# Seven half products for eight in the gate and up blocks of a SwiGLU, with their sums on three engines

## The chip, the cores and the metric

One core of a Trainium2 chip runs the whole program. The metric is the device time of one execution in microseconds (us), as the median of several runs. The profile is of one execution of its own; the time from its first to its last instruction is called the span.

The engines go by the profile's names. PE is the matrix engine, and PEld its loading of the stationary operand, which runs beside the products. DVE is the vector engine, ACT the scalar engine with the activation functions, POOL is GpSimd, and SP issues the transfers (DMA). SBUF is the memory in which tiles of 128 partitions lie; PSUM holds the eight banks that PE writes its sums to, each 128 x 512 float32.

## What is computed

One decoder layer on 512 tokens of width 1024: a SwiGLU, a token mixer (short convolution and sparse attention side by side), a second SwiGLU, a final norm. Scale, shift and gate vectors come from a conditioning vector `c` by a matrix `w_ada`. All arithmetic is to the accuracy of float32.

```python
D_MODEL = 1024; SEQ = 512; D_FF = 2816
def _swiglu(h, w_gate, w_up, w_down):
    return (jax.nn.silu(h @ w_gate) * (h @ w_up)) @ w_down
# in the layer
mod = (silu(c) @ w_ada + b_ada).reshape(B, 9, D_MODEL)      # shift, scale, gate, three times
h = _modulate(_rmsnorm(x, g_ffn1), sh1, sc1)
x = x + 0.5 * gt1 * _swiglu(h, w1_gate, w1_up, w1_down)
h = _modulate(_rmsnorm(x, g_mix), sh2, sc2)
x = x + gt2 * _hybrid_mixer(h, ...)
h = _modulate(_rmsnorm(x, g_ffn2), sh3, sc3)
x = x + 0.5 * gt3 * _swiglu(h, w2_gate, w2_up, w2_down)
return _rmsnorm(x, g_final)
```

## The kernel before

Channels lie on the partitions: `x`, and `h` in eight blocks of 128 channels by 512 tokens. Each operand of a product is kept as a high and a low part (`hhi`, `hlo`; `whi`, `wlo`; `ghi`, `glo`), and `mm3` (L280) makes one product out of three: high by high, high by low, low by high.

The 22 blocks `f` of 128 hidden channels of a SwiGLU have a gate and an up column block each. Blocks 0 to 2 are made together as `h` comes, channel block by channel block, in products of 256 tokens (`first_group`, and `first_products` in the first SwiGLU). Every later one is made by two calls of `project` (L536), gate then up, each 8 channel blocks x 3 products of 512 tokens into one bank. `glu` (L593) then takes the silu on ACT, multiplies by the up bank on DVE (L600), and splits the result on ACT (L605) and DVE (L607). After blocks 0 to 10 the first half of the last product is made (`part`, 8 channel blocks of the output, each 11 x 3 products) and added to `x` (`first_half`, L628); then come blocks 11 to 21 and the second half. Of that second half the last two output blocks are made in halves of 256 tokens, first both for tokens 0 to 255, then both for the rest, so that the norm of the first half of the tokens runs under the products of the second.

Weights come in units of 128 x 1024: SP loads a unit to one of four `raw` tiles (L344), ACT makes `whi` of it (L366), DVE or POOL makes `wlo` = `raw` - `whi` (L355). There are four pairs of `whi` and `wlo`. Under the first SwiGLU the other seven conditioning vectors are made (`ada_loads`, `ada_sums`): 56 rows of 128 x 1024 of `w_ada` are loaded to three `araw` tiles, and each is scaled and added on DVE (L862, L865); four small products and two transposes on PE end a vector.

What stands in which order on each engine is decided when the program is built. `Plan` is a list scheduler: a task asks for an engine and a time, or for one of several (`low_part` asks for DVE, or for POOL at a tax), and the plan takes the task that could begin first, with ranks for ties. Its costs are the functions from L218 on. Each engine then runs its instructions strictly in that order, and waits where an operand is not there.

Of the kernel before, what the change touches and what calls it, by code (L numbers as in the profile page):

```python
# [19 lines left out]
P = 128  # L20
# [5 lines left out]
FH = FK // 2  # L26
# [14 lines left out]
# columns of the packed per-channel vectors  # L41
# [8 lines left out]
# columns of the packed constants  # L50
# [74 lines left out]
class Slots:  # L125
    """Tokens for memory that is used over and over."""
# [108 lines left out]
def c_ptt(n):  # L235
    return POOL, 0.25 + 2.0e-3 * n
# [19 lines left out]
def tile_hymba_layer(ctx: ExitStack, tc: tile.TileContext, xT, pos, cols_d, con_d, wa0, wa1, f1a, f1b, f1d,  # L256
# [1636 lines left out]
```

## Time and profile before

| what | value |
|---|---|
| median of 3 runs | 1082.68 us (1081.89 to 1084.97) |
| span of the profiled execution | 1081.2 us |
| PE busy | 1062.0 us (98%), 5417 products |
| DVE busy | 606.7 us (56%) |
| ACT busy | 409.9 us (38%) |
| POOL busy | 49.8 us (5%) |
| granted clock of PE, mean | 0.989 of full speed |
| transferred by DMA | 133.60 MB, mean 124 GB/s |

The stages by the trace: up to about 66 us the start with the first vectors and the first products, to about 418 us the first SwiGLU, to about 700 us the mixer, to 1071 us the second SwiGLU, and then the final norm. Durations of matrix products in the rows overlap, since they are pipelined: what one costs is the distance from its start to the next start. The same holds, to a smaller degree, for back to back instructions of DVE, whose rows overlap by some 0.08 us.

### The profile page before, as it was taken

To read this page: it belongs to the slowest core of one execution; us is meant where nothing else is said; L and a number is where in the kernel's file an instruction comes from. 1 tells how busy PE (TensorE), PEld (TensorE's weight loads), DVE (VectorE), ACT (ScalarE), POOL (GpSimd) and SP (SyncE) were. 2 spreads that over 40 slices of the span, in tenths; PEclk is the share of its full clock that TensorE was granted. 3 is DMA by queue.
4 is the path that set the end of the run, shared out by engine and by line. 5 is a ranking of instruction groups with operands and counts; after the bars stand their busy time and mean duration, and the time that the engine had idled before them with its cause. 6 is when DMAs were issued, how large, how long until landed. Compare 5 with 4: busy or idle time off the path is not lost.

```text
span 1081.2 us, 13889 instructions
## 1 busy us (share of the span) xinstructions
PE 1062.0 (98%) x5417; PEld 860.6 (80%) x5417; DVE 606.7 (56%) x1069; ACT 409.9 (38%) x713; POOL 49.8 (5%) x47
## 2 busy tenths in 40 slices
PE   8999999999999999999999999999999999999997
PEld 5777677788888889987777777998888888888887
DVE  4978888833333347499787786654333323333334
ACT  4552222212222233358756785334222122222321
POOL 0310000000000001012001010100000000000000
PEclk8999999999999999999999999999999999999998
DMA  9659989532222230443300003224333333322302
GB/s 333 243 191 326 315 322 327 176 96 85 92 98 98 98 103 16 131 125 122 127 25 28 13 14 96 92 83 132 94 89 91 98 98 98 94 86 93 98 20 78
DMA packets 40706, 133.60 MB, mean 124 GB/s; under 512 B 4704, under 2 KB 8032, under 8 KB 40000
## 3 DMA queue, kind: packets, MB, share of 16 engines
q1 hardware_dynamic: 40640, 132.71, 37.3%
q8 instruction: 42, 0.69, 0.3%
q14 instruction: 24, 0.20, 0.1%
HBM read 130.14 MB, written 2.10 MB: 122 GB/s over the span
## 4 chain that ended last, share of the span: by engine, by line
PE 88%; DVE 5%; DMA 4%; issue 1%; ACT 0%; SPq 0%; DVEq 0%; ACTq 0%
PE b L278 86%; DMA araw<-in_wa_dram 3%; PE b L1396 2%; DVE ada L865 1%; DVE afirst L736 1%; DVE wlo L355 1%; DMA x<-in_xT_dram 1%; DVE s L519 1%; DMA raw<-in_f1b_dram 0%; PE b L1291 0%; DVE afirst L733 0%; DVE v L393 0%; PE b L1241 0%; DVE afirst L728 0%; ACT hhi L523 0%
## 5 line engine op out<-in xcount | busy, mean ns | idle before, releaser
L278 PE MATMUL b<-hhi,whi 128*128 128x512 f32 (+1 forms) x1020 | 386.1, 379 | 0.0
L278 PE MATMUL b<-hlo,whi 128*128 128x512 f32 (+1 forms) x1020 | 379.0, 372 | 0.5 <-DVE hlo L525 0.4
L278 PE MATMUL b<-hhi,wlo 128*128 128x512 f32 (+1 forms) x1020 | 378.7, 371 | 0.0
L366 ACT ACTIVATE whi<-raw 128x1024 fp32r<-128x1024 f32 (+3 forms) x176 | 178.1, 1013 | 461.8 <-PE b L278 319.8
L355 DVE TENSOR_TENSOR wlo<-raw,whi 128x1024 fp32r<-128x1024 f32 (+3 forms) x162 | 191.2, 1180 | 218.4 <-ACT whi L366 213.0
L278 PEld LDWEIGHTS b<-hhi,whi 128*128 128x128 f32 x1020 | 192.3, 189 | 41.5 <-issue 6.7
L278 PEld LDWEIGHTS b<-hhi,wlo 128*128 128x128 f32 x1020 | 192.5, 189 | 36.6
L278 PEld LDWEIGHTS b<-hlo,whi 128*128 128x128 f32 x1020 | 192.7, 189 | 34.9 <-DVE hlo L525 1.2
L278 PE MATMUL b<-ghi,whi 128*128 128x512 f32 (+1 forms) x364 | 138.2, 380 | 0.0
L278 PE MATMUL b<-ghi,wlo 128*128 128x512 f32 (+1 forms) x364 | 137.4, 378 | 0.0
L278 PE MATMUL b<-glo,whi 128*128 128x512 f32 (+1 forms) x364 | 137.4, 378 | 0.0
L600 DVE TENSOR_TENSOR s<-sg,b 128x512 f32<-128x512 f32 x44 | 30.1, 686 | 106.6 <-PE b L278 105.8
L278 PEld LDWEIGHTS b<-ghi,whi 128*128 128x128 f32 x364 | 68.4, 188 | 14.7 <-issue 0.8
L278 PEld LDWEIGHTS b<-ghi,wlo 128*128 128x128 f32 x364 | 68.5, 188 | 14.0
L278 PEld LDWEIGHTS b<-glo,whi 128*128 128x128 f32 x364 | 68.5, 188 | 13.9
L865 DVE SCALAR_TENSOR_TENSOR ada<-araw,cact,ada 128x1024 f32<-128x1024 f32 x49 | 66.7, 1360 | 16.8 <-DMA araw<-in_wa_dram 16.1
L532 DVE SCALAR_TENSOR_TENSOR x<-b,mod,x 128x512 f32<-128x512 f32 (+1 forms) x30 | 19.1, 643 | 42.3 <-PE b L278 42.3
L450 ACT ACTIVATE s<-x 128x256 f32<-128x256 f32 (+1 forms) x41 | 19.4, 491 | 56.8 <-DVE x L532 53.7
L355 POOL TENSOR_TENSOR wlo<-raw,whi 128x768 fp32r<-128x768 f32 (+2 forms) x14 | 30.8, 2197 | 217.8 <-ACT whi L366 162.8
L605 ACT ACTIVATE ghi<-s 128x512 fp32r<-128x512 f32 x44 | 27.5, 631 | 15.7 <-DVE s L600 15.7
L523 ACT ACTIVATE hhi<-s,mod 128x256 fp32r<-128x256 f32 (+1 forms) x42 | 20.8, 533 | 31.5 <-DVE s L519 28.5
L1407 DVE TENSOR_TENSOR PT<-b,PT 128x384 fp32r<-128x384 f32 (+1 forms) x48 | 28.2, 598 | 5.0 <-ACT PT L1405 4.5
(238 smaller groups left out, 969.0 us busy)
## 6 DMA issues: line engine op xcount, KB each, us to landing
araw<-in_wa_dram SPq DMA_DIRECT2D x56, 512.0 KB
raw<-in_f1b_dram SPq DMA_DIRECT2D x38, 512.0 KB
raw<-in_f2b_dram SPq DMA_DIRECT2D x38, 512.0 KB
raw<-in_f1d_dram SPq DMA_DIRECT2D x22, 512.0 KB
raw<-in_f2d_dram SPq DMA_DIRECT2D x22, 512.0 KB
raw<-in_wib_dram SPq DMA_DIRECT2D x14, 512.0 KB
wfirst<-in_wa_dram SPq DMA_DIRECT2D x5, 1024.0 KB
raw<-in_wc_dram SPq DMA_DIRECT2D x8, 512.0 KB
```

Source lines behind the costliest of these rows:

```text
L278: nc.tensor.matmul(o, lhsT, rhs, start=start, stop=stop)
L355: (nc.vector if e == DVE else nc.gpsimd).tensor_sub(wlo_of[j][:, :n], raw_of[i][:, :n], whi_of[j][:, :n].bitcast(F32))
L366: nc.scalar.activation(whi_of[j][:, :n], raw_of[raw_at[u]][:, :n], AF.Copy)
L450: nc.scalar.activation(o[:, ts], x[d][:, ts], AF.Square)
L519: nc.vector.scalar_tensor_tensor(t, x[d][:, ts], am[:, s, d:d + 1], rb(), op0=OP.mult, op1=OP.mult)
L523: nc.scalar.activation(hhi[d][:, ts], t, AF.Identity, bias=sh)
L532: nc.vector.scalar_tensor_tensor(x[d][:, ts], bank_of[b][:, ts], gate, x[d][:, ts], op0=OP.mult, op1=OP.add)
L600: nc.vector.tensor_mul(scr_of[q], sg_of[k], bank_of[bu])
L605: nc.scalar.activation(ghi[j], scr_of[q], AF.Copy)
L865: nc.vector.scalar_tensor_tensor(a, w, cact[:, k:k + 1], a, op0=OP.mult, op1=OP.add)
L1396: nc.tensor.transpose(pt[:, w:w + P], Pr[t][:, kb * P:(kb + 1) * P], ident)
L1407: nc.vector.tensor_sub(pl[:, :w], pt[:, :w], ph[:, :w].bitcast(F32))
```

## The change

From block 6 on in the first SwiGLU and from block 5 on in the second, 33 blocks in all, gate and up are made together by `seven`. Split `h` into its even and odd channel blocks and into tokens 0 to 255 (A) and 256 to 511 (B): gate and up are then a product of a 2 x 2 by a 2 x 2 of half blocks, eight half products, which Winograd's form of Strassen's method makes with seven products and sums of operands and results. Each of the seven is 4 channel blocks x 3 parts, 12 products of 256 tokens.

- The sums of `h` (`build_t`, tiles `thi`, `tlo`) are made once for each SwiGLU.
- The sums of the weights (`sums`, `sum_parts`, tiles `wsh`, `wsl`, four half slots) are made for every block: four sums of 512, and three splits of 512 into parts.
- The sums of results (`collect` in `seven`) are one copy of 256 on ACT and five additions of 256 on DVE for every block.
- The last product is made in four groups of 6, 6, 5 and 5 blocks for two of 11, each of the first three added to `x` as a whole. One more block of gate and up is made before each.
- In `ada_sums` the rows of `w_ada` come as 112 halves of 512, with three `araw` tiles of half the size; ACT scales a half and DVE or POOL adds it, or DVE does both at once.
- In the plan, POOL's cost of a subtraction is raised from 0.25 + 2.0e-3 n to 0.3 + 2.3e-3 n, its tax for weight work from 0.5 to 2, and PE's cost of three products is now 3 x (0.1133 + 0.469e-3 (n - 256)). Two kept unit slots are made at the end of the second SwiGLU as well.

Removed comments are left out here; so are the classes and loops that only carry the new units.

```diff
-FH = FK // 2
+SIZES = (6, 6, 5, 5)
+PLAIN = (6, 6, 5)
+def _steps():
+    for g in range(len(SIZES)):
+        for f in range(max(GROUP[g], GRP), GROUP[g + 1]):
+            yield "f", f
+            if g and f == GROUP[g]:
+                yield "d", g - 1
+    yield "d", len(SIZES) - 1
...
 def c_ptt(n):
-    return POOL, 0.25 + 2.0e-3 * n
+    return POOL, 0.3 + 2.3e-3 * n
...
 def c_mm3(n):
-    return PE, 3 * max(n / 2370, 0.105)
+    return PE, 3 * (0.1133 + max(0, n - 256) * 0.469e-3)
...
+    def sums(p):
+        a, b = p.u, p.u + 1
+        yield loaded[a]
+        yield loaded[b]
+        ga, up = raw_of[raw_at[a]], raw_of[raw_at[b]]
+        E, O = slice(0, T), slice(T, 2 * T)
+        x = yield scr
+        s1 = scr_of[x]
+        e = yield c_tt(T), (*c_ptt(T), W_TAX)
+        either(e).tensor_add(s1, up[:, E], up[:, O])
+        e = yield c_tt(T), (*c_ptt(T), W_TAX)
+        either(e).tensor_sub(up[:, E], ga[:, E], up[:, E])
+        done(p.third)
+        go(R_W, sum_parts(p, "1", s1, scr, x))
+        yield made[a]
+        e = yield c_tt(T), (*c_ptt(T), W_TAX)
+        either(e).tensor_sub(ga[:, E], s1, ga[:, E])
+        p.freed(scr, x, give)
+        go(R_W, sum_parts(p, "2", ga[:, E], raws, raw_at[a]))
+        e = yield c_tt(T), (*c_ptt(T), W_TAX)
+        either(e).tensor_sub(ga[:, O], ga[:, O], ga[:, E])
+        go(R_W, sum_parts(p, "4", ga[:, O], raws, raw_at[a]))
+
+    def sum_parts(p, n, v, slots, at):
+        p.slot[n] = yield halves_
+        hi, lo = half(p.slot[n])
+        yield c_act(T)
+        nc.scalar.activation(hi, v, AF.Copy)
+        e = yield c_tt(T), (*c_ptt(T), W_TAX)
+        either(e).tensor_sub(lo, v, hi.bitcast(F32))
...
+        def build_t(e):
+            x0, x1 = (yield scr), (yield scr)
+            h0, h1 = scr_of[x0], scr_of[x1]
+            for o, d in ((h0, 2 * e), (h1, 2 * e + 1)):
+                q = yield c_tt(T), (*c_ptt(T), W_TAX)
+                either(q).tensor_add(o, hhi[d].bitcast(F32), hlo[d].bitcast(F32))
+            a0, b0, a1, b1 = h0[:, A], h0[:, B], h1[:, A], h1[:, B]
+            for o, v, w in ((a0, b0, a0), (b0, b1, b0), (b1, b1, a0), (a1, a1, b1)):
+                q = yield c_tt(T // 2), (*c_ptt(T // 2), W_TAX)
+                either(q).tensor_sub(o, v, w)
+            for i, x in enumerate((x0, x1)):
+                hi, lo = (v[e][:, i * T:(i + 1) * T] for v in (thi, tlo))
+                yield c_act(T)
+                nc.scalar.activation(hi, scr_of[x], AF.Copy)
+                q = yield c_tt(T), (*c_ptt(T), W_TAX)
+                either(q).tensor_sub(lo, scr_of[x], hi.bitcast(F32))
...
+        def seven(f):
...
+            def collect(by):
...
+                yield has[1]
+                yield c_act(T // 2)
+                nc.scalar.activation(v, X[:, A], AF.Copy)
+                done(has["copied"])
+                yield has[6]
+                yield c_tt(T // 2)
+                nc.vector.tensor_add(v, v, Y[:, A])
+                yield has[7]
+                yield c_tt(T // 2)
+                nc.vector.tensor_add(w, v, Y[:, B])
+                done(has["w"])
...
+                nc.vector.tensor_add(up[:, B], w, X[:, B])
+                done(has["up"])
...
+                nc.vector.tensor_add(up[:, A], v, Y[:, B])
...
+                nc.vector.tensor_add(X[:, B], v, X[:, B])
+                give(scr, q)
+                k = yield from silu(f, bx)
+                e = yield c_tt(T), (*c_ptt(T), W_TAX)
+                either(e).tensor_mul(up, up, sg_of[k])
+                give(sgs, k)
+                yield from parts(f, r)
...
+            yield made[a]
+            yield from product(X[:, A], unit(a, 0), first(0, A), True)
+            done(has[1])
...
+            yield from product(Y[:, A], summed("2"), t_of(2), True)
...
+            yield from product(Y[:, B], unit(b, 0), t_of(3))
...
+            yield from product(X[:, B], summed("1"), t_of(1))
...
+            yield has["copied"]
+            yield from product(X[:, A], unit(a, DK // 2), first(1, A))
+            free_unit(a)
+            yield has["w"]
+            yield from product(Y[:, B], unit(b, DK // 2), t_of(4))
...
+            yield has["up"]
+            yield from product(X[:, B], summed("4"), first(1, B))
...
-                nc.vector.tensor_scalar(a, w, cact[:, 0:1], None, op0=OP.mult)
+                yield ACT, c_act(T)[1]
+                nc.scalar.activation(a, w, AF.Copy, scale=cact[:, 0:1])
             else:
-                yield c_stt(D)
-                nc.vector.scalar_tensor_tensor(a, w, cact[:, k:k + 1], a, op0=OP.mult, op1=OP.add)
+                e = yield c_stt(T), c_act(T)
+                if e == DVE:
+                    nc.vector.scalar_tensor_tensor(a, w, cact[:, k:k + 1], a, op0=OP.mult, op1=OP.add)
+                else:
+                    nc.scalar.activation(w, w, AF.Copy, scale=cact[:, k:k + 1])
+                    e = yield c_tt(T), (*c_ptt(T), W_TAX)
+                    either(e).tensor_add(a, a, w)
```

How this stands on the engines is shown at three places, each by a piece of the order before and of the order after. A number behind a name is that of the buffer.

PE, in the middle of the first SwiGLU. Before, the end of one `project` and the start of the next, 512 tokens each:

```order
L278 MATMUL b0_63<-hlo7_120,whi3_96 128x512
L278 MATMUL b0_63<-hhi7_112,wlo3_100 128x512
L278 MATMUL b6_69<-hhi0_105,whi0_93 128x512
L278 MATMUL b6_69<-hlo0_113,whi0_93 128x512
L278 MATMUL b6_69<-hhi0_105,wlo0_97 128x512
L278 MATMUL b6_69<-hhi1_106,whi0_93 128x512
```

After, the end of the first of seven half products and the start of the second, with sums of `h` and of weights as operands:

```order
L753 MATMUL b6_69<-hhi4_109,whi2_95 128x256
L753 MATMUL b6_69<-hlo4_117,whi2_95 128x256
L753 MATMUL b6_69<-hhi4_109,wlo2_99 128x256
L753 MATMUL b6_69<-hhi6_111,whi2_95 128x256
L753 MATMUL b6_69<-hlo6_119,whi2_95 128x256
L753 MATMUL b6_69<-hhi6_111,wlo2_99 128x256
L753 MATMUL b1_64<-thi0_679,wsh0_687 128x256
L753 MATMUL b1_64<-tlo0_683,wsh0_687 128x256
L753 MATMUL b1_64<-thi0_679,wsl0_688 128x256
L753 MATMUL b1_64<-thi1_680,wsh0_687 128x256
L753 MATMUL b1_64<-tlo1_684,wsh0_687 128x256
L753 MATMUL b1_64<-thi1_680,wsl0_688 128x256
```

A block has 48 products of 512 tokens before and 84 of 256 tokens after.

DVE, in the middle of the first SwiGLU. Before, between the L600 of one block and that of the next, with most of the time on rows of `w_ada` (L862, L865):

```order
L600 TENSOR_TENSOR s4_75<-sg0_688,b0_63 128x512
L865 SCALAR_TENSOR_TENSOR ada0_661<-araw0_658,cact_101,ada0_661 128x1024
L607 TENSOR_TENSOR glo6_683<-s4_75,ghi6_672 128x512
L865 SCALAR_TENSOR_TENSOR ada0_661<-araw1_659,cact_101,ada0_661 128x1024
L865 SCALAR_TENSOR_TENSOR ada0_661<-araw2_660,cact_101,ada0_661 128x1024
L355 TENSOR_TENSOR wlo0_97<-raw0_89,whi0_93 128x1024
L862 TENSOR_SCALAR ada1_662<-araw0_658,cact_101 128x1024
```

After, part of one block: weight sums (L422 to L433), their low parts (L442), sums of results (L782, L785, L791), the product of up and silu (L803) and its low part (L722), and halves of `w_ada` (L1115):

```order
L429 TENSOR_TENSOR raw2_91<-s5_76,raw2_91 128x512
L1115 TENSOR_TENSOR ada0_661<-ada0_661,araw2_660 128x512
L803 TENSOR_TENSOR s3_74<-s3_74,sg1_678 128x512
L433 TENSOR_TENSOR raw2_91<-raw2_91 128x512
L782 TENSOR_TENSOR s4_75<-s4_75,b1_64 128x256
L722 TENSOR_TENSOR glo3_674<-s3_74,ghi3_668 128x512
L442 TENSOR_TENSOR wsl1_690<-s5_76,wsh1_689 128x512
L785 TENSOR_TENSOR s4_75<-s4_75,b1_64 128x256
L1115 TENSOR_TENSOR ada0_661<-ada0_661,araw0_658 128x512
L422 TENSOR_TENSOR s1_72<-raw1_90 128x512
L791 TENSOR_TENSOR s2_73<-s4_75,b0_63 128x256
```

Weight sums, result sums and the rows of `w_ada` now stand in turns in DVE's one queue.

POOL. Before, from the end of the start to the mixer, it has two subtractions under the first SwiGLU (the last two here), and next a memset of the mixer:

```order
L355 TENSOR_TENSOR wlo2_99<-raw2_91,whi2_95 128x768
L728 TENSOR_TENSOR afirst1_133<-afirst1_133 128x256 x2
L355 TENSOR_TENSOR wlo0_97<-raw0_89,whi0_93 128x1024
L355 TENSOR_TENSOR wlo3_100<-raw3_92,whi3_96 128x1024
L996 MEMSET swp0_2754 128x512
```

After, a piece of the first SwiGLU, in which it has 11 of 1024 and 20 of 512:

```order
L396 TENSOR_TENSOR wlo1_98<-raw1_90,whi1_94 128x1024
L422 TENSOR_TENSOR s2_73<-raw1_90 128x512
L396 TENSOR_TENSOR wlo3_100<-raw2_91,whi3_96 128x1024
L442 TENSOR_TENSOR wsl0_688<-s5_76,wsh0_687 128x512
L442 TENSOR_TENSOR wsl0_688<-raw3_92,wsh0_687 128x512
L396 TENSOR_TENSOR wlo1_98<-raw0_89,whi1_94 128x1024
L442 TENSOR_TENSOR wsl1_690<-s1_72,wsh1_689 128x512
L442 TENSOR_TENSOR wsl0_688<-raw1_90,wsh0_687 128x512
L396 TENSOR_TENSOR wlo3_100<-raw3_92,whi3_96 128x1024
```

About one low part of a unit and one or two of a weight sum have gone from DVE to POOL for every block in this stretch.

## Rows read from the trace of the kernel before

**Rows 1.** The page's first part: busy us (share of the span) and instructions.

```profile
PE 1062.0 (98%) x5417; PEld 860.6 (80%) x5417; DVE 606.7 (56%) x1069; ACT 409.9 (38%) x713; POOL 49.8 (5%) x47
```

**Rows 2.** Windows from:to, length: busy us (instructions) by engine, PEclk, DMA share, GB/s.

```profile
core 0: us, PE busy (x) PEld busy (x) DVE busy (x) ACT busy (x) POOL busy (x), PEclk, DMA share, GB/s
100.00:165.00 65.00, 62.70 (x280) 48.67 (x279) 54.80 (x54) 17.86 (x24) 2.58 (x1) 0.97 0.90 314
205.00:300.00 95.00, 95.00 (x409) 76.55 (x408) 35.79 (x42) 24.87 (x31) 0.00 (x0) 1.00 0.29 95
427.00:705.00 278.00, 277.61 (x1624) 221.78 (x1623) 216.62 (x545) 170.81 (x366) 27.09 (x22) 1.00 0.24 75
705.00:1066.00 361.00, 361.00 (x1731) 298.72 (x1731) 129.88 (x161) 102.36 (x132) 0.00 (x0) 1.00 0.29 88
```

**Rows 3.** Timeline of PE: start, duration, instruction; 512 tokens, then 256.

```profile
399.69 0.39 PE L278 MATMUL b<-ghi,wlo 128*128 128x512 f32 x1
...
402.03 0.28 PE L278 MATMUL b<-ghi,whi 128*128 128x256 f32 x1
...
402.94 0.28 PE L278 MATMUL b<-ghi,wlo 128*128 128x256 f32 x1
```

**Rows 4.** Timeline of PE near the end of the second SwiGLU.

```profile
1061.04 0.28 PE L278 MATMUL b<-ghi,whi 128*128 128x256 f32 x1
...
1061.98 0.28 PE L278 MATMUL b<-ghi,wlo 128*128 128x256 f32 x1
```

**Rows 5.** Groups by line and shape: operation, count | busy us, mean ns | idle before.

```profile
L355 DVE TENSOR_TENSOR wlo<-raw,whi 128x1024 fp32r<-128x1024 f32 x136 | 166.3, 1224 | 188.9 <-ACT whi L366 183.5 <-PE b L278 0.8
L865 DVE SCALAR_TENSOR_TENSOR ada<-araw,cact,ada 128x1024 f32<-128x1024 f32 x49 | 66.7, 1360 | 16.8 <-DMA araw<-in_wa_dram 16.1
L463 DVE TENSOR_TENSOR ssum<-ssum,s 128x256 f32<-128x256 f32 x18 | 7.6, 423 | 6.6 <-ACT s L450 6.1
```

**Rows 6.** Timeline of DVE, back to back instructions in the first SwiGLU.

```profile
84.88 0.68 DVE L600 TENSOR_TENSOR s<-sg,b 128x512 f32<-128x512 f32 x1
85.47 1.22 DVE L355 TENSOR_TENSOR wlo<-raw,whi 128x1024 fp32r<-128x1024 f32 x1
86.61 0.69 DVE L607 TENSOR_TENSOR glo<-s,ghi 128x512 fp32r<-128x512 f32 x1
87.21 2.60 DVE L865 SCALAR_TENSOR_TENSOR ada<-araw,cact,ada 128x1024 f32<-128x1024 f32 x2
89.73 1.22 DVE L355 TENSOR_TENSOR wlo<-raw,whi 128x1024 fp32r<-128x1024 f32 x1
```

**Rows 7.** Timelines of POOL and of DVE around POOL's two subtractions of the first SwiGLU.

```profile
76.19 2.40 POOL L355 TENSOR_TENSOR wlo<-raw,whi 128x1024 fp32r<-128x1024 f32 x1 [18.63 <-ACT whi L366]
119.07 2.58 POOL L355 TENSOR_TENSOR wlo<-raw,whi 128x1024 fp32r<-128x1024 f32 x1 [40.48 <-ACT whi L366]
...
76.62 3.05 DVE L865 SCALAR_TENSOR_TENSOR ada<-araw,cact,ada 128x1024 f32<-128x1024 f32 x1 [0.57 <-DMA araw<-in_wa_dram]
79.59 0.68 DVE L607 TENSOR_TENSOR glo<-s,ghi 128x512 fp32r<-128x512 f32 x1
...
118.09 4.64 DVE L865 SCALAR_TENSOR_TENSOR ada<-araw,cact,ada 128x1024 f32<-128x1024 f32 x2 [1.74 <-DMA araw<-in_wa_dram]
```

**Rows 8.** The same two engines in the mixer, where DVE's operation reads a bank.

```profile
679.22 1.87 POOL L355 TENSOR_TENSOR wlo<-raw,whi 128x768 fp32r<-128x768 f32 x1 [35.53 <-PE b L278]
...
679.18 2.85 DVE L532 SCALAR_TENSOR_TENSOR x<-b,mod,x 128x512 f32<-128x512 f32 x4 [2.48 <-PE b L278]
```

**Rows 9.** Groups of POOL: the smallest subtraction of weights.

```profile
L355 POOL TENSOR_TENSOR wlo<-raw,whi 128x640 fp32r<-128x640 f32 x2 | 3.1, 1566 | 21.1 <-ACT whi L366 21.1
```

**Rows 10.** Waits of DVE from 66 to 210: us in total, times, longest.

```profile
DVE ada L865 <- DMA araw<-in_wa_dram: 16.1, 20, 2.1
DVE ada L862 <- DMA araw<-in_wa_dram: 2.7, 3, 1.7
```

**Rows 11.** Timeline of DVE at the end of the first SwiGLU.

```profile
410.47 0.48 DVE L532 SCALAR_TENSOR_TENSOR x<-b,mod,x 128x256 f32<-128x256 f32 x1 [3.01 <-PE b L278]
412.22 0.16 DVE L483 TENSOR_SCALAR v<-b 128x2 f32<-128x2 f32 x1 [1.27 <-PE b L278]
...
415.23 1.25 DVE L519 SCALAR_TENSOR_TENSOR s<-x,am,b 128x256 f32<-128x256 f32 x3
```

More of the change, by code (lines that the diff above doesn't have):

```diff
@@ L353, in low_part, with half, either @@
         n, i, j = units[u].shape[-1], raw_at[u], w_at[u]
-        e = yield c_tt(n), (*c_ptt(n), POOL_TAX)
+        e = yield c_tt(n), (*c_ptt(n), W_TAX)
         (nc.vector if e == DVE else nc.gpsimd).tensor_sub(wlo_of[j][:, :n], raw_of[i][:, :n],
                                                           whi_of[j][:, :n].bitcast(F32))
-        give(raws, i)
+        if u not in pair_of or u != pair_of[u].u:
+            give(raws, i)
         done(made[u])
+    half_of, halves_ = [], Slots()
+    def half(i):
+        t, c = divmod(i, 2)
+        return tuple(v[:, c * T:(c + 1) * T] for v in half_of[t])
+    def either(e):
+        return nc.vector if e == DVE else nc.gpsimd
+    def sums(p):
[27 more added lines that the diff above has]
+        either(e).tensor_sub(lo, v, hi.bitcast(F32))
+        p.freed(slots, at, give)
+        done(p.made[n])
     def make_units():
@@ L362, in make_units @@
             yield loaded[u]
+            p = pair_of.get(u)
+            if p is not None and u == p.u:
+                go(R_W, sums(p))
+            elif p is not None:
+                yield p.third
             j = yield slots_of.get(u, ws)
@@ L602, in glu @@
             give(sgs, k)
-            j = yield gs[f % FH]
-            yield c_act(T)
-            nc.scalar.activation(ghi[j], scr_of[q], AF.Copy)
-            yield c_tt(T)
-            nc.vector.tensor_sub(glo[j], scr_of[q], ghi[j].bitcast(F32))
-            give(scr, q)
-            done(g_in[f])
-        def part(half, d, b, ts, keep=False):
-            for k in range(FH):
-                n = d * FH + k
-                if (half, n // 8) not in at:
-                    at[half, n // 8] = take_unit()
-                u = at[half, n // 8]
+            yield from parts(f, q)
@@ L617, in part @@
+        def part(g, d, b, ts, keep=False):
+            m = SIZES[g]
+            for k in range(m):
+                n = d * m + k
+                if (g, n // 8) not in at:
+                    at[g, n // 8] = take_unit()
+                u = at[g, n // 8]
                 yield made[u]
-                yield g_in[half * FH + k]
+                yield g_in[GROUP[g] + k]
                 yield c_mm3(ts.stop - ts.start)
-                mm3(bank_of[b][:, ts], cols(u, n % 8), (ghi[k][:, ts], glo[k][:, ts]), k == 0, k == FH - 1)
+                mm3(bank_of[b][:, ts], cols(u, n % 8), (ghi[k][:, ts], glo[k][:, ts]), k == 0, k == m - 1)
@@ L629, in first_half, with keep @@
             give(banks, b)
+        def keep():
+            for k in range(N_S):
+                yield halves_
+            for hi, lo in half_of:
+                whi_of.append(hi)
+                wlo_of.append(lo)
+                give(kept[s], len(whi_of) - 1)
         def main():
@@ L653, in main @@
                     b = yield banks
-                    yield from part(1, d, b, ts, True)
+                    yield from part(last, d, b, ts, True)
                     go(R_X, residual(d, b, gate[d], ts, norm))
-            for n in range(8, FH):
-                free_unit(at[1, n])
+            for n in range((DK - 2) * SIZES[last] // 8, SIZES[last]):
+                free_unit(at[last, n])
             done(end)
+        for e in range(DK // 2):
+            go(R_T, build_t(e))
         go(R_MAIN, main())
```

194 lines of the change are left out of this document (147 added, 47 removed).

## The prediction

> **What bounds the kernel now.** I read the busy shares first, then the windows by stage, then the distances between starts on PE and on DVE. PE is busy for 98% of the span [rows 1], and in both SwiGLUs it is busy without a gap: 95.0 of 95.0 us from 205 to 300, 361.0 of 361.0 us from 705 on, at a granted clock of 1.00 [rows 2]. Fewer products there should therefore shorten the end, as long as the other engines keep up. DVE has room in these windows (36 of 95 us, 130 of 361), but little from 100 to 165 us, where the rows of `w_ada` are added: 54.8 of 65 us, with the transfers at 90% [rows 2]. That stretch is where the change puts most of its new work, so it decides.
>
> **Products.** Ten products of 512 tokens lie between 399.69 and 402.03, 0.234 us each; the eight of 256 after them take 0.91 us, 0.114 each [rows 3]. Other stretches of 256 run slower: 1061.04 to 1061.98 is eight of them, 0.1175 each [rows 4]. A block goes from 48 x 0.234 = 11.23 us to 84 x 0.114 = 9.58 (gain 1.65) or to 84 x 0.1175 = 9.87 (gain 1.36). The 33 blocks give 54.5 or 44.9 us. What tells the two speeds apart I can't see in the rows, so I take the middle, 1.50 a block: 24 us in the first SwiGLU (16 blocks), 25.5 in the second (17). The last product in four groups has the same number of products, so PE pays nothing for it; its 32 more additions to `x` go to DVE.
>
> **DVE in the first SwiGLU.** From start to start, DVE takes 1.14 us for 1024, 0.60 for 512 (85.47 to 86.61 to 87.21) and half of 2.52/2 = 1.26 for a half row scaled and added at once, 0.63 [rows 6]. For 256 I take the mean of 0.42 less the overlap of 0.08 that 1024 shows (1.22 against 1.14): 0.34 [rows 5, 6]. An addition to `x` is 2.85/4 = 0.71 [rows 8]. In the order after, I counted the stretch from block 7 to block 17, with one group of the last product in it. DVE has 20 of 1024, 130 of 512, 13 half rows, 54 of 256 and 9 additions to `x`: 22.8 + 78.0 + 8.2 + 18.4 + 6.4 = 133.8 us, and nine single operations for the rotary tables, some 4 us (estimate, below the 0.60 each). PE has 11 x 9.58 + 144 x 0.234 = 139 us there. So DVE alone is full, at 138 of 139 us, and the plan could only get there by giving POOL 8 of 1024 and 13 of 512.
>
> **What POOL's share costs.** The rows speak against counting it as free. POOL ran a subtraction from 76.19 to 78.59; DVE's L865, next at 76.62, took 3.05 us for a usual 1.3, and DVE's following start was at 79.59, a full operation after POOL's end. The same happened at 119.07: two L865 took 4.64 us for 2.5 [rows 7]. DVE waits, then, until POOL is through. Where DVE reads a bank it doesn't: four L532 at 679.18 ran in 2.85 us under POOL's 1.87 [rows 8].
>
> The Trainium skill, "SBUF — State Buffer", section "Who interferes with whom", has this as a rule: a DVE instruction with two SBUF inputs and a GpSimd instruction that reads SBUF exclude each other for the whole instruction, whichever came first, and a DVE instruction with at most one SBUF input outside its two-port modes is free. By that rule the sums here, which nearly all read two SBUF tiles, gain nothing from going to POOL; the trace's 3.05 us at 76.62 agrees.
>
> POOL's 1024 takes 2.40 us when it runs first [rows 7]; 640 takes 1.57 [rows 9], so 512 some 1.3 (estimate on the line through both). In the stretch: 8 x 2.40 + 13 x 1.3 = 36 us. DVE's operations that read a bank are 18.4 + 6.4 = 25 of its 138 us, 18%, and can pass under POOL; so I put 82% of the 36 on DVE's queue, 30 us, which PE then waits for. DVE may be ahead by half a block (four weight slots and four half slots are two blocks' at most), 5 us: 25 us of stall. Ends: half of POOL's time hidden and the same lead, 13; all of it and no lead, 36. Before block 7 the account is even: blocks 3 to 5 ask 29 + 11 us of DVE and POOL against 33 of PE, the group behind them gives that back. After block 17 DVE has room (28.8 against 38 us for the last four blocks), but a stall once paid isn't returned. If the 256 products are the slow ones, the stall shrinks by as much as PE loses.
>
> **The second SwiGLU** has no rows of `w_ada`, and POOL gets 15 operations. At its start the sums of `h` meet blocks 3 and 4 and the first seven: 4 of 1024, 34 of 512 and 20 of 256 are 31.8 us of DVE, with 2 x 2.4 + 4 x 1.3 = 10 of POOL, against 31.9 of PE. I charge 6 us (2 to 10). Later the six blocks 7 to 12 ask 47.4 us of DVE and 4 of POOL against 57.5: covered, with 6 us to spare.
>
> **Ends of the SwiGLUs.** The norm of tokens 0 to 255 runs under the products for the other half: two output blocks of 11 x 3 x 0.1175 = 3.9 us, 7.8 in all, now 5 x 3, 3.5 in all: 4.2 us less cover. The chain behind it took 410.47 to 415.23, 4.8 us, before `h` could be built [rows 11]. At the first end PE then waits for some 3 us; at the second, where the norm's first half and the last stores lie closer together, I take 1.5. Both from 0 to 4.
>
> **Waits inside a block.** Of the seven products, the sixth and the seventh wait for sums on DVE that begin two products earlier, 2.3 us; two additions of 0.34 fit unless a 1.14 or a POOL lock is in front. I charge 2 us over all blocks (0 to 6). Mixer code is the same; the plan's changed costs may order it otherwise. It has PE at 277.6 of 278 us by the modelled ends, with DVE at 217 [rows 2]: 0, from -4 to 4.
>
> **Sum**, against the profiled span of 1081.2: -49.5 + 25 + 6 + 4.5 + 2 = -12, 1069.2. The median lies 1.5 us above that span: 1071. The measurement can tell a change of over 0.3%, 3.2 us. The forecast's own range takes the ends together: from -54.5 + 13 + 2 + 3 = -36.5 to -44.9 + 36 + 10 + 7 - 10 (slow products hide a part of the stall) = -2: 1046 to 1081.
>
> **Rivals.**
> 1. POOL's work is hidden after all, for instance since DVE often waits for something else in that time. Then the stall in the first SwiGLU is DVE's alone (138 against 139, some 3 us), and 2 in the second: -49.5 + 5 + 6.5 = -38, with fast products -43: 1038 to 1046. For: POOL is the smaller of the two. Against: [rows 7], every time. 0.15.
> 2. Slower: a full DVE queue that waits for `w_ada`. Before, its L865 and L862 waited 18.8 us for transfers, nearly all that L865 ever waited [rows 5, 10], and PE felt little of it since DVE had room. Now a half row passes from DMA to ACT to DVE with half as many bytes in flight, and behind a late one stand the low parts and weight sums that PE's next product needs. If these waits come again and nothing covers them, they are added whole: -12 + 19 = 7, 1090. It turns slower once over 12 us of them reach PE. Against: ACT had 18 of 65 us to do there [rows 2], and the faster half of `w_ada`'s time now has longer to run. 0.17.
> 3. In between, within 3.2 us of before: the stall at its upper end, some of those waits. 0.13.
> 4. That the products don't get shorter: each of 256 has a weight load of its own. Within [rows 3] they did run at 0.114 with one load each, so this has no chance of its own.
>
> **How the numbers follow.** The forecast has 0.55, rival 1 0.15, so faster 0.70; same 0.13; slower 0.17. The range leaves out some 0.12 below and 0.08 above: 1043 to 1092.
>
> **What would show it.** Right: PE gaps in the first SwiGLU of about 25 us, before products that wait for L396, L442 or the additions of `collect`; the second SwiGLU about 15 us shorter than before, with its gaps at its start; DVE operations of 0.60 that last 1.5 to 2.5 us wherever POOL runs. Wrong: POOL and DVE overlapping on two SBUF inputs (rival 1); DVE idle before L1115 or L1111 with ACT or DMA as the releaser (rival 2); products of 256 at over 0.12.

## The result, and the profile after

The changed kernel takes 1090.95 us (median, 1089.57 to 1092.42), the kernel before, run beside it, 1083.83. The ratio is 1.0072, 95% interval 1.0052 to 1.0091: slower, where 1071 and faster were forecast. The profiled execution has a span of 1090.6 us for 1081.2.

Page, first part, after (for [rows 1]):

```profile
PE 1040.3 (95%) x6533; PEld 900.1 (83%) x6533; DVE 861.9 (79%) x1565; ACT 559.8 (51%) x969; POOL 117.9 (11%) x79
```

PE is busy for 22 us less, but the span is longer: it now idles. In what follows f6 is block 6, a pair is a block whose gate and up are made together by `seven`, and a group is one of the four parts of the last product. Stages, from the first product of each to the first of the next, in us; "undisturbed" is the time of the same products where nothing waits. In the first SwiGLU blocks 0 to 2 take products of 256 tokens for their first two channel blocks alone; the first row begins with the first product of 512, which still belongs to them:

| stage | before | after | undisturbed |
|---|---|---|---|
| first SwiGLU, first product of 512 to the last product's end | 382.8 | 395.3 | |
| of it f6 (first pair) | | 17.8 | 9.96 |
| of it f7 to f12, a group, f13 to f17 | | 77.6 + 34.6 + 58.5 | 59.8 + 33.6 + 49.8 |
| of it f18 to f21 | | 39.8 | 39.8 |
| from there to the second SwiGLU's first product (the mixer) | 281.1 | 284.7 | |
| second SwiGLU | 371.0 | 363.4 | |
| of it f5 and f6 (first pairs) | | 31.4 | 19.9 |
| of it f7 to f21 | | 59.8 + 49.8 + 39.8 | the same |

A pair, undisturbed, takes 9.96 us, a block before 11.2. Windows after (for [rows 2]; from:to, length, busy us of PE, PEld, DVE, ACT, POOL, then PEclk, DMA share, GB/s):

```profile
101.10:118.90 17.80, 13.36 (x85) 12.32 (x83) 13.41 (x21) 11.52 (x17) 0.00 (x0) 0.81 0.70 235
159.40:236.90 77.50, 69.05 (x525) 65.26 (x524) 74.26 (x107) 46.07 (x71) 25.09 (x12) 0.93 0.57 189
271.50:330.10 58.60, 53.68 (x432) 52.00 (x431) 55.57 (x82) 35.67 (x57) 16.73 (x8) 0.97 0.61 202
772.20:803.60 31.40, 22.70 (x170) 22.29 (x169) 23.55 (x33) 13.76 (x21) 4.19 (x3) 0.84 0.30 101
837.20:897.00 59.80, 59.80 (x506) 59.80 (x505) 49.78 (x80) 30.35 (x43) 7.64 (x3) 1.00 0.31 107
```

From f7 to f17 DVE is busy nearly all the time (74.3 of 77.5, 55.6 of 58.6), time in which it waits for POOL inside an operation included. Where no row of `w_ada` passes, last line, it has 49.8 of 59.8 us, and PE never waits. What PE waits for, over the whole span (us, times, longest):

```profile
PE b L753 <- DVE s L785: 8.4, 6, 3.0
PE b L300 <- DVE ada L1115: 7.7, 7, 1.8
PE b L753 <- DVE wsl L442: 6.7, 2, 6.0
PE b L753 <- ACT s L778: 4.7, 3, 3.7
```

L785 is `collect`'s second sum, L442 a low part of a weight sum. The waits are short, but the longer ones cost more than their length. After the 2.95 us at 291.68 the products start 0.11 us apart until 293.21, and 0.21 from there; the granted clock of 291.68 to 295.50 is 0.69, so part of it ran at the lower of the two levels, 1.2 GHz for 2.4 (PE's timeline):

```profile
291.68 0.39 PE L753 MATMUL b<-thi,whi 128*128 128x256 f32 x1 [2.95 <-DVE s L785]
291.90 0.28 PE L753 MATMUL b<-tlo,whi 128*128 128x256 f32 x1
...
293.80 0.41 PE L753 MATMUL b<-hhi,wsl 128*128 128x256 f32 x1
294.02 0.41 PE L753 MATMUL b<-hhi,wsh 128*128 128x256 f32 x1
```

Added over all starts of f7 to f12, 11.3 us are gaps and 5.4 us such doubled distances.

On the other engines three things stand in front of these waits. First, POOL and DVE exclude each other, as in [rows 7]: a subtraction of 0.60 lasts 1.79 beside POOL's.

```profile
175.35 1.54 POOL L442 TENSOR_TENSOR wsl<-raw,wsh 128x512 fp32r<-128x512 f32 x1 [1.37 <-ACT wsh L440]
175.66 1.79 DVE L433 TENSOR_TENSOR raw<-raw 128x512 f32<-128x512 f32 x1
```

Second, in f6 PE's last wait is for ACT's queue. The fourth product waits for ACT's copy of the first result (L778). The first product had ended at 102.6, but the copy stands behind a row of `w_ada`, for which ACT waits on the DMA (compare [rows 10]), and behind three other operations:

```profile
106.72 0.72 ACT L1113 ACTIVATE araw<-araw,cact 128x512 f32<-128x512 f32 x1 [1.19 <-DMA araw<-in_wa_dram]
107.35 0.58 ACT L713 ACTIVATE sg<-b 128x512 f32<-128x512 f32 x1
107.83 1.04 ACT L457 ACTIVATE whi<-raw 128x1024 fp32r<-128x1024 f32 x1
109.35 0.63 ACT L720 ACTIVATE ghi<-s 128x512 fp32r<-128x512 f32 x1 [0.48 <-DVE s L730]
109.88 0.36 ACT L778 ACTIVATE s<-b 128x256 f32<-128x256 f32 x1
...
110.30 0.58 PE L753 MATMUL b<-thi,wsh 128*128 128x256 f32 x1 [3.66 <-ACT s L778]
```

Third, at the second SwiGLU's start two of POOL's operations hold up DVE in a row, L433 and then L442, so that the low part at 782.18 reaches PE 6 us late:

```profile
775.36 2.35 POOL L396 TENSOR_TENSOR wlo<-raw,whi 128x1024 fp32r<-128x1024 f32 x1 [2.83 <-ACT whi L457]
775.40 2.85 DVE L433 TENSOR_TENSOR raw<-raw 128x512 f32<-128x512 f32 x1
...
779.31 1.75 DVE L442 TENSOR_TENSOR wsl<-s,wsh 128x512 fp32r<-128x512 f32 x1
...
782.18 0.68 DVE L442 TENSOR_TENSOR wsl<-raw,wsh 128x512 fp32r<-128x512 f32 x1
...
782.92 0.58 PE L753 MATMUL b<-thi,wsl 128*128 128x256 f32 x1 [6.04 <-DVE wsl L442]
```

### The profile page after: what moved, and what is told of

Its sections match the earlier page's. It is cut to its first block, busy times and chain, and to the rows that moved or that the text cites. A ratio compares the mean times of both kernels' runs of the same rounds, so it can differ in the third digit from the quotient of the medians.

```text
span 1090.6 us, 17104 instructions
## 1 busy us (share of the span) xinstructions
PE 1040.3 (95%) x6533; PEld 900.1 (83%) x6533; DVE 861.9 (79%) x1565; ACT 559.8 (51%) x969; POOL 117.9 (11%) x79
## 4 chain that ended last, share of the span: by engine, by line
PE 59%; DVE 8%; issue 2%; DMA 1%; ACT 1%; SPq 0%; ACTq 0%; DVEq 0%
PE b L300 38%; PE b L753 19%; PE b L1646 2%; DVE wlo L396 1%; DMA araw<-in_wa_dram 1%; DVE s L700 1%; DVE tlo L706 1%; DVE blkf L1357 1%; DVE glo L722 0%; DVE s L696 0%; DVE wsl L396 0%; DMA raw<-in_f1d_dram 0%; PE b L1541 0%; DVE wsl L442 0%; DVE raw L429 0%
## 5 line engine op out<-in xcount | busy, mean ns | idle before, releaser
L300 PE MATMUL b<-hhi,whi 128*128 128x512 f32 (+1 forms) x492 | 175.3, 356 | 2.2 <-ACT hhi L614 2.1
L300 PE MATMUL b<-hlo,whi 128*128 128x512 f32 (+1 forms) x492 | 169.8, 345 | 1.0 <-DVE hlo L616 0.9
L300 PE MATMUL b<-hhi,wlo 128*128 128x512 f32 (+1 forms) x492 | 169.4, 344 | 0.0
L300 PE MATMUL b<-ghi,whi 128*128 128x512 f32 x320 | 128.1, 400 | 1.3 <-ACT ghi L720 1.3
L300 PE MATMUL b<-glo,whi 128*128 128x512 f32 x320 | 127.2, 398 | 0.8 <-DVE glo L722 0.8
L300 PE MATMUL b<-ghi,wlo 128*128 128x512 f32 x320 | 127.2, 397 | 0.0
L300 PEld LDWEIGHTS b<-hhi,whi 128*128 128x128 f32 x492 | 92.5, 188 | 17.8 <-issue 3.5
L300 PEld LDWEIGHTS b<-hlo,whi 128*128 128x128 f32 x492 | 93.1, 189 | 12.0 <-DVE hlo L616 2.2
L300 PEld LDWEIGHTS b<-hhi,wlo 128*128 128x128 f32 x492 | 92.4, 188 | 12.3
L753 PE MATMUL b<-thi,whi 128*128 128x256 f32 x264 | 76.8, 291 | 8.5 <-DVE s L785 8.4
L1115 DVE TENSOR_TENSOR ada<-ada,araw 128x512 f32<-128x512 f32 x87 | 69.2, 796 | 15.1 <-ACT araw L1113 15.1
```

Source lines behind the costliest of these rows:

```text
L300: nc.tensor.matmul(o, lhsT, rhs, start=start, stop=stop)
L753: nc.tensor.matmul(o, u, v, start=start and not e and not i, stop=e == DK // 2 - 1 and i == 2, skip_group_check=not start)
L1115: either(e).tensor_add(a, a, w)
```

## Experiments: what fills DVE

Theory A: POOL's exclusion of DVE makes the stall. Theory B: DVE has more to do than fits beside the products, wherever it is done. Theory C: the waits for rows of `w_ada` make it.

**POOL does no weight work.**

```diff
-W_TAX = 2
+W_TAX = 1000
```

> GpSimd takes none of the weights' work any more (its planned cost there is put out of reach); DVE does all of it, products and blocks stay as changed. Theory A (a GpSimd operation on two SBUF inputs and a DVE operation of that kind cannot run side by side, so GpSimd's share is paid on DVE with interest): in the stretch of the pairs f7 to f12 DVE was busy for 73.7 of 77.5 us, 15.7 of it longer than its own operations last elsewhere, while GpSimd had 12 operations; on DVE these would be some 12 to 17 us of 512-wide rows' time halved, about 8 to 10 us. So DVE's load falls to about 66 to 68, the stretch to about the same (from 77.5), that of f13 to f17 from 58.5 to 50 to 52, and the start of the second SwiGLU by 3 to 5 us: 1066 to 1074. Theory B (DVE is too full and GpSimd relieves it): DVE takes 8 + 6 + 8 us more in these three stretches and the kernel is slower, 1103 to 1113. Theory C (the stall is the wait for the rows of w_ada through ACT): 1088 to 1094.

Measured: 1087.18 us, 1.0037 (1.0019 to 1.0056) of before; the interval just meets that of the change. The profile is of an execution of 1083.8 us, one of the faster of ten. Windows of f6, f7 to f12 and f13 to f17, and, from f7 to f17, what PE waited for, and what DVE waited for most (us, times, longest):

```profile
107.80:118.90 11.10, 10.99 (x93) 10.23 (x92) 8.62 (x14) 8.05 (x13) 0.00 (x0) 1.00 0.82 273
153.70:230.30 76.60, 66.05 (x525) 64.15 (x524) 68.06 (x117) 50.03 (x78) 0.00 (x0) 0.93 0.63 200
264.90:326.70 61.80, 54.31 (x442) 52.61 (x441) 55.92 (x95) 38.94 (x61) 0.00 (x0) 0.94 0.57 180
```

```profile
PE b L753 <- DVE wsl L442: 18.0, 6, 5.8
DVE s L782 <- PE b L753: 11.9, 8, 2.7
```

f7 to f17 takes 173.0 us for 170.7. So A fails as the cause: without POOL nothing excludes DVE, and the stall is the same. A's figure for DVE's load from f7 to f12 did come out, 68.1 us for 66 to 68, but the stretch took 76.6. B fails with its number too: POOL was no relief. What it took from DVE it gave back as waiting. C's 1088 to 1094 is the nearest; the next runs test it. DVE's own work from 153.7 to 326.7 is 157.7 us (68.1, 33.7 in the group between, 55.9), beside 143.2 us of undisturbed products. That load is about half of the 29.8 us lost (an estimate, 157.7 less 143.2). For the rest of the time DVE itself idles, 15.3 us, mostly in front of a sum of results (L782) that waits for PE, while PE waits for a low part (L442) further back in DVE's queue; and the clock is at 0.93 and 0.94. No run changed the order in DVE's queue alone, so how much of the stall is load and how much is order stays open. The second SwiGLU's first pairs do run in 19.9 us for 31.4, but its plain blocks lose 5.1 (27.5 us for 22.4).

**Without the sums of `w_ada`**, and, apart from it, **without the sums of the pairs**.

```diff
-            if k == 0:
+            if k and k < DK - 1:
+                pass
+            elif k == 0:
```

Of the eight rows of a group the middle six are loaded, but not added.

> As changed, but of the rows of w_ada that pass through DVE and ACT in the first SwiGLU only the first and the last of the eight of each group are summed (so the modulations are other numbers; loads and reductions stay). DVE's load in f7 to f12 falls by about 18 of 27 additions of 0.69 to 0.9 us, some 14 to 20 us, and in f13 to f17 by about 14. Theories A and B alike: no stall is left in the pairs of the first SwiGLU (59.8 for 77.5, 49.8 for 58.5, 9.96 for the 17.8 of f6): 1055 to 1062; A alone would leave a few us where GpSimd still works beside DVE. If the pairs' stall has to do with TensorE's own speed or the halves' buffers: 1085 or more.

Measured: 1086.03 us. The total misses the 1055 to 1062 by far, and by its number falls to the last alternative, that the stall has to do with PE or the buffers; the stage speaks against that: f13 to f17 has no stall left (DVE 40.4 of 49.9), while f7 to f12 still takes 74.7.

```profile
163.90:238.60 74.70, 68.22 (x536) 64.59 (x535) 60.73 (x99) 36.99 (x57) 9.95 (x4) 0.95 0.77 248
275.10:325.00 49.90, 49.90 (x422) 49.85 (x421) 40.39 (x65) 24.82 (x35) 4.48 (x2) 1.00 0.33 106
```

Its waits are others, though: they are before the small products that end a vector of `w_ada`. With less to add, the plan probably puts these earlier than the transfers can bring the rows (argued, not tested); from 160 to 238, PE waits for these and hardly for a pair (us, times, longest):

```profile
PE b L300 <- DVE ada L1113: 4.2, 2, 2.2
...
PE b L753 <- DVE s L782: 0.8, 1, 0.8
```

That run had taken away C's cause together with B's. The next keeps the rows and leaves out the pairs' sums:

```diff
+    def light(p):
+        return DK + 14 < p.u < n_ffn
...
-        e = yield c_tt(T), (*c_ptt(T), W_TAX)
-        either(e).tensor_add(s1, up[:, E], up[:, O])
+        if not light(p):
+            e = yield c_tt(T), (*c_ptt(T), W_TAX)
+            either(e).tensor_add(s1, up[:, E], up[:, O])
```

(the other three sums and the split in the same way; it holds for f8 to f21 of the first SwiGLU, which compute with leftover numbers)

> As changed (pairs from f6 and f5 on), but in the first SwiGLU the pairs f8 to f21 use leftover numbers for their sums: the four sums of half units and the three subtractions that split them are left out, so DVE and GpSimd have 7 operations of 512 fewer a pair (about 4.2 us of 9.4), and the blocks' results are other numbers; ACT's copies, the rows of w_ada, the loads and the products stay. If the stall is DVE's load, sums of pairs and rows of w_ada together over what fits beside 9.96 us of products, then taking away the sums is as good as taking away w_ada: f13 to f17 in 50 to 51 us for 58.5, f7 to f12 in 62 to 66 for 77.6 (f7 still has its sums), 1068 to 1073 in all. If it is the rows of w_ada by themselves, DVE's queue waiting for them through ACT: 75 and more, 57 and more, 1086 to 1091.

Measured: 1067.28 us, 0.9867 (0.9848 to 0.9885). f7 to f12 and f13 to f17:

```profile
154.20:217.10 62.90, 62.14 (x523) 60.52 (x522) 57.37 (x100) 47.43 (x75) 0.00 (x0) 1.00 0.70 227
252.60:304.20 51.60, 50.90 (x432) 50.22 (x431) 39.66 (x66) 35.56 (x55) 0.00 (x0) 1.00 0.70 222
```

62.9 and 51.6, about as the load predicts (62 to 66, 50 to 51), with every row of `w_ada` still passing through ACT or DVE. So C fails from f7 to f17: there it is pairs and `w_ada` together in DVE's queue that PE waits for, and either alone fits. With the sums POOL's work in this stretch has gone as well, but the run without POOL showed that POOL isn't needed for the stall.

f6 keeps its 17.8 us here, with the wait of 3.65, since its sums and those of `h` are still made. That ACT's queue is the cause of it is not borne out: without most of the additions of `w_ada` the stretch from the first product of 512 to f6's end is no shorter. The runs below point to the sums of `h`, which are made in front of f6.

## Experiments: where pairs pay

**The groups alone, and pairs in the second SwiGLU alone.**

```diff
-PLAIN = (6, 6, 5)
+PLAIN = (22, 22, 22)
...
-            go(R_T, build_t(e))
+            if PLAIN[s] < 22:
+                go(R_T, build_t(e))
```

The second run has `PLAIN = (22, 22, 5)`.

> No block in seven anywhere; what is left of the change is the last product in four groups of (6, 6, 5, 5), the rows of w_ada in halves, and the order of the columns. My sum put the ends at 3 us and some 1.5 for the rest: 1084 to 1088. If the groups themselves stall (weights of the last product or the sums of w_ada late): above 1090. If the halved rows of w_ada help by themselves: 1078 to 1083.

> Seven half products only in the second SwiGLU; the first computes its blocks f3 to f21 in eight and builds no sums of h, but keeps the four groups and the half rows of w_ada. If the loss is what the pairs put on DVE in the first SwiGLU while the rows of w_ada pass through it (Theories A and B alike): the first SwiGLU is back near 383 to 387 us instead of 395.3, the second keeps its 363 us: 1076 to 1082, faster than the kernel before. If it is the four groups or the halved rows of w_ada that cost the first SwiGLU its time: 1088 to 1094.

Measured: 1087.33 us, 1.0043 (1.0024 to 1.0061), for the groups alone, and 1078.62, 0.996 (0.9944 to 0.9976), for the second alone. What the change adds beside the pairs costs some 5 us, close to the 4.5 that the forecast put on the ends; the run doesn't tell the ends from the groups and the half rows. In the second run the first SwiGLU takes 381.2 us over the stretch of the table (395.3 as changed), the second stalls at f5 and f6 as before (31.1 us). The second run makes no sums of `h` in the first SwiGLU, and there PE waits nowhere from 60 to 120:

```profile
60.00:120.00 60.00, 60.00 (x264) 47.58 (x263) 40.52 (x56) 35.03 (x51) 0.00 (x0) 1.00 0.74 236
```

**Pairs where DVE has room.** From f18 in the first, from f7 in the second; then the same without POOL, with the sums of `h` of the first SwiGLU built later, and with one pair more.

```diff
-PLAIN = (6, 6, 5)
+PLAIN = (18, 18, 7)
...
         def build_t(e):
+            if s == 0:
+                yield g_in[13]
```

The second run also has `W_TAX = 1000`; the second piece comes with the third; the fourth has `PLAIN = (18, 18, 6)`.

> Seven half products only from f18 on in the first SwiGLU (where the rows of w_ada are through) and from f7 on in the second (two blocks more than before between the building of the sums of h and the first pair). If the pairs cost nothing wherever DVE has room, this is the kernel with pairs in the second SwiGLU only (1078.6), less 4 blocks x 1.24 us in the first, less the 11.5 us stall at the second's start, plus the 2 x 1.24 us that the two plain blocks give up: 1064.6, within 1062 to 1068. If the first two pairs of a SwiGLU stall wherever they stand (an empty pipeline of sums and not the collision with the sums of h): 1072 to 1077. If the building of the sums of h in the first SwiGLU costs what it did where no GpSimd was used (the 512-wide blocks f3 to f5 took 5 us more): 1069 to 1071.

> The same places for the pairs, and GpSimd takes none of the weights' work. Where DVE has room the split should not matter: within 2 us of the kernel with late pairs. If GpSimd's operations still cost DVE time that the products then wait for: 2 to 6 us faster than it. If DVE's relief is still needed at the starts: 3 to 8 us slower.

> Late pairs, and the sums of h of the first SwiGLU are built only when block f13 is done instead of at its start, beside the first blocks. With late pairs the stretch of f3 to f6 took 85.9 us, 77.8 where no sums of h are built. If those 8 us are DVE's work on the sums of h (four times 3.9 us) ahead of the parts that products wait for: 78 in that stretch and 1065 to 1067. If they come back before f18, where DVE still sums rows of w_ada: 1069 to 1074.

> As the run with later sums of h, and the second SwiGLU's pairs begin with f6 instead of f7. If the 11.5 us stall at f5 and f6 came from the sums of h (15.6 us of DVE) meeting the first pairs' sums within two plain blocks, 11.2 us more of plain block are enough for most of it: 1.2 us less to 3 us more than that run. If a pair ahead of the first part of the last product stalls as such: 5 us more and above.

Measured: 1073.88 us, 0.9912 (0.9894 to 0.9931); 1079.33, 0.9964 (0.9947 to 0.9981); 1064.74, 0.9821 (0.9788 to 0.9854); 1064.58, 0.9839 (0.9815 to 0.9864). The second SwiGLU stalls nowhere in the first, third and fourth; the fourth's f6 takes 9.9 us, so a first pair costs nothing by itself. The first run was above its 1068 because of the stretch up to f6, where the sums of `h` stood in front; the third mended that. The windows from the first product of 512 to the end of f6, which is no pair in either, first and third run:

```profile
34.00:119.90 85.90, 77.94 (x334) 59.88 (x333) 74.92 (x114) 47.15 (x81) 18.50 (x10) 0.96 0.56 188
```

```profile
33.40:111.40 78.00, 75.47 (x334) 58.67 (x333) 57.98 (x90) 42.29 (x72) 4.97 (x4) 1.00 0.68 217
```

So the 8 us are lost at f6 with the sums of `h` in front even where f6 is no pair (20.5 us for 11.2), and not without them, while rows of `w_ada` pass through ACT in both.

Without POOL it was slower, not the same: in the second SwiGLU's plain blocks PE waited 3.23 us for a `wlo` of DVE. There POOL is a relief. The third and fourth run beat the kernel before by 1.8% and 1.6%, and the changed one, which did not run beside them, by about 2.4%; between them there is no difference that can be measured.

## Experiments: POOL beside DVE, and the distance of products

**Three operations of POOL more in each of the 15 pairs of the second SwiGLU**, on top of the late pairs; with two SBUF inputs, then with one.

```diff
+            nc.gpsimd.tensor_sub(idle_of, v, thi[1][:, :T].bitcast(F32))
...
+            for i in range(3 if s else 0):
+                go(R_W, beside(whi_of[w_at[a]][:, :T].bitcast(F32)))
```

In the second run the first line is `nc.gpsimd.tensor_scalar(idle_of, v, 0.5, None, op0=OP.mult)`.

> Late pairs, and in each of the 15 pairs of the second SwiGLU three more GpSimd subtractions of 128x512 with two SBUF inputs, whose result nobody reads; DVE's and TensorE's work is unchanged. There DVE was busy 49.8 of 60 us (8.3 us a block). If a GpSimd operation of this kind makes DVE's wait (15.7 us longer for 25.2 us of GpSimd in the first SwiGLU, 0.62 for 1): 3 x 1.5 x 0.62 = 2.8 us a block more on DVE, 11.1 for TensorE's 9.96, so 15 to 20 us more than with late pairs, 1080 to 1085, with DVE rows of 2 us and more beside the GpSimd rows. If the two work side by side and the long rows had other reasons: no change.

> As the run with 45 more GpSimd subtractions, but each is a multiplication of 128x512 by a constant, with one SBUF input instead of two. If it is GpSimd's two-input operations that make DVE wait: DVE's rows keep their lengths and the time is that with late pairs, 1073.9 within 1.5 us. If any GpSimd operation on SBUF does it: 3 x 0.7 us a block, 1.3 to 2.1 us more on DVE, and 2 to 8 us more in all.

Measured, a single execution each: 1087.54 and 1075.47 us, against 1073.88 (1073.41 to 1075.90) without. The first is above the 1080 to 1085 that were expected; the second can't be told from the run without. f7 to f12 with late pairs, with two inputs, with one:

```profile
819.30:879.10 59.80, 59.80 (x506) 59.80 (x505) 49.79 (x80) 30.21 (x43) 6.94 (x3) 1.00 0.33 106
```

```profile
815.20:882.80 67.60, 62.64 (x506) 61.32 (x505) 62.07 (x85) 29.78 (x43) 23.30 (x13) 0.97 0.29 94
```

```profile
819.70:880.20 60.50, 60.41 (x505) 59.93 (x504) 52.50 (x83) 30.21 (x43) 25.11 (x13) 1.00 0.32 105
```

With two inputs POOL is busy for 16.4 us more and DVE for 12.3; with one, 18.2 and 2.7. In both runs three weight sums (L422) that POOL made in the window of late pairs fall to DVE, some 1.9 us of it, so the price of the added operations themselves is about 10 us and 1 us (estimates). Rows of the first of them (DVE's two L442 take 1.2 elsewhere):

```profile
833.58 4.74 POOL L742 TENSOR_TENSOR beside<-whi,thi 128x512 f32<-128x512 f32 x3 [4.25 <-ACT whi L457]
833.74 1.70 DVE L424 TENSOR_TENSOR raw<-raw,raw 128x512 f32<-128x512 f32 x1
835.36 3.51 DVE L442 TENSOR_TENSOR wsl<-raw,wsh 128x512 fp32r<-128x512 f32 x2
```

Rows of the second: POOL's three operations in a row, and a subtraction of DVE with two SBUF inputs (0.68 elsewhere) in the midst of them.

```profile
828.13 6.02 POOL L742 TENSOR_SCALAR beside<-whi 128x512 f32<-128x512 f32 x3 [6.88 <-ACT whi L457]
829.48 0.77 DVE L429 TENSOR_TENSOR raw<-s,raw 128x512 f32<-128x512 f32 x1
```

So the exclusion of two inputs by two inputs is real and costs PE time; theory A had the mechanism, but not the cause of the stall.

**Distances**, on late pairs: products 1 and 6, and 7 and 5, written in turn; and, on the run with later sums of `h`, the half tiles placed first in their pool.

```diff
+            yield from products((X[:, A], unit(a, 0), first(0, A), True), (Y[:, A], summed("2"), t_of(2), True))
...
+            yield from products((Y[:, B], unit(b, 0), t_of(3), False), (X[:, B], summed("1"), t_of(1), False))
```

> Late pairs as before, but the half products 1 and 6, and 7 and 5, are written in turn, three multiplications of the one and three of the other, so that consecutive triples go to two banks. If the distance of 0.118 to 0.120 us between starts (0.114 in the first group of a SwiGLU) comes from twelve multiplications in a row into the same half bank, 48 of 84 fall to about 0.114: 19 blocks x 48 x 0.005 = 4.6 us less than with late pairs, 1060 for 1064.6. If it comes from where the weights lie or from the moved operand changing with every triple, the distances stay at 0.118 and 0.120 and the time within 1 us, or 1 to 4 us more where product 1 must now wait for the sum that product 6 reads.

> As the run with later sums of h; only the tiles of the four half units (wsh, wsl) are placed ahead of the others of their pool instead of behind them. If the 0.120 us between starts for these weights (0.1175 for whi and wlo) is a matter of the tile's place: another distance, 0.1175 at best, 36 x 0.0025 x 19 = 1.7 us less. If it is something else: 0.120 again and the same time.

Measured: 1106.33 us, 1.0196 (1.017 to 1.0223), and 1062.33 (a single execution, within the 1060.13 to 1067.82 of the run without it). In both the starts stay 0.117 to 0.118 us apart with `whi` and `wlo`, 0.120 with `wsh` and `wsl`: neither the banks in turn nor the tiles' place sets them. The order in turn is far worse than was expected of it (1060 to 1069), probably since the results now come two products later and nothing covers the sums. PE's waits for its pairs of the second SwiGLU:

```profile
PE b L758 <- DVE s L790: 11.4, 9, 1.5
PE b L758 <- ACT s L783: 7.1, 15, 0.5
```

## Why the prediction was wrong

Three terms of the sum had the wrong size, and all erred the same way, by 21.4 us together: the products by 8.6, the stall in the first SwiGLU by 7.3, the start of the second by 5.5. By the forecast's own terms, against the span, in us:

| term | forecast | measured |
|---|---|---|
| 33 blocks shorter | -49.5 | -40.9 (33 x 1.24) |
| stall in the first SwiGLU | +25 | +32.3 (12.5 longer, and 16 x 1.24 gained) |
| start of the second | +6 | +11.5 (31.4 - 19.9) |
| ends, waits inside blocks, mixer | +6.5 | +6.5 (what is left of 9.4) |
| sum | -12 | +9.4 |

- **Products.** The middle of two speeds was taken; undisturbed pairs ran at the slow one of [rows 4], and their products with the new tiles slower still. Nor did the stall shrink by what PE lost, as the forecast said it would: f7 to f17 lost 27.5 us beside pairs of 9.96. Starts of three products in a row, after: 844.25, 845.66 and 847.10, so 12 products with `whi` and `wlo` take 1.41 us, 12 with `wsh` and `wsl` 1.44.

```profile
844.25 0.28 PE L753 MATMUL b<-thi,whi 128*128 128x256 f32 x1
...
845.66 0.28 PE L753 MATMUL b<-hhi,wsh 128*128 128x256 f32 x1
...
847.10 0.28 PE L753 MATMUL b<-hhi,whi 128*128 128x256 f32 x1
```

- **Stall in the first SwiGLU.** From f7 to f17 it was close: 27.5 us lost (170.7 for 143.2). What failed is "before block 7 the account is even", and that nothing was put down behind block 17: f6 lost 7.8 us, the group behind it 6.1 (39.7 for 33.6), and the group behind f17 2.9 (30.9 for 28.0). Against these 16.8 us the kernel before lost 9.7 from 89.1 to 165.9 (76.9 us for products of 67.2); the rest is smaller. At f6 the account took the sums of `h` too lightly, to which the runs with late pairs point. The lower clock behind the longer gaps was not in the sum.
- **Rival 2.** Its waits came: from 66 to 210 DVE idled 11.9 us before L1115 and L1111 for halves of `w_ada`. But from f7 to f17 it was 1.4 us, so they didn't make the stall there. That its sign and its 1090 came out is luck.
- **Its reason** was half right. POOL's work comes back as waiting, as said. Rival 1 falls with the rows that show it, 1.79 us for 0.60; the run without POOL is no test of its "DVE's alone (138 against 139, some 3 us)", since there POOL's share, some 17 us by the forecast's costs (8 x 1.14 + 13 x 0.60), is added to the 138, close to the 157.7 measured. What the reason missed is that the stall comes without any exclusion too: counted as the forecast counts, DVE's work over PE's, that run would have lost 14.5 us, and it lost 29.8.
- **Start of the second.** 31.8 us of DVE and 10 of POOL against 31.9 of PE, read as in the first SwiGLU (82% of POOL's time on DVE), would have given some 8 for the 6. The rest is the place: the exclusions sit directly in front of the first pairs' low parts, and the clock over these 31.4 us is 0.84. Without POOL 5.1 us were lost at this start.
- **Right:** the pairs elsewhere without a stall, and the place and kind of the gaps; the ends in so far as what is left over comes to the forecast's sum (3.6 us of it lie between the two SwiGLUs, where nothing tells the end from the mixer). The range, 1043 to 1092, held the time; the sign did not hold, since three terms erred the same way.

## What to carry to other kernels

Fewer products are worth their gain only where the engine that pays for them has that time free: here the same pairs gained 1.24 us each in stretches with DVE at 83%, and lost more than that where another stream already used it. Put the new work by stretch, not by kernel; here that made 1.8% faster out of 0.7% slower, with the same products and sums at other places. A busy share below one doesn't yet mean that the work fits: in a queue with a fixed order, one operation that waits holds up those behind it. Work that is handed to POOL with two SBUF inputs must be counted on DVE as well, unless DVE is idle then.

## What the runs showed of the hardware

- DVE and POOL exclude each other also the other way round: POOL's subtraction of 1024 at 756.54 lasted 7.07 us (2.40 in [rows 7]), while DVE went through twelve operations, most with two SBUF inputs, back to back.

```profile
756.54 7.07 POOL L396 TENSOR_TENSOR wlo<-raw,whi 128x1024 fp32r<-128x1024 f32 x1 [23.19 <-ACT whi L457]
```

- With one SBUF input POOL's operations, though as long, made DVE busy for 2.7 us more, not 12.3; about 1 and 10 without the sums that moved to DVE (estimates above). The Trainium skill, "SBUF — State Buffer", section "Who interferes with whom", lets a DVE instruction with two SBUF inputs contend with any GpSimd instruction that reads SBUF; the run with two inputs agrees, the run with one input hardly does.
- A gap of 3 us on PE was followed by a stretch at half speed: 0.21 us between starts from 293.21 on, after the one at 291.68. Over f7 to f12 that made 5.4 us on top of 11.3.
- What sets the distance of 256-token products (0.114, 0.118 or 0.120 us) stays open.
